# In-place low halves of q and k, u in the ring of x with R made per block, x issued by ScalarE, and one store of v for two heads

## The chip, the cores and the metric

The kernel runs on one core of a Trainium2 chip. The metric is the device time of one launch in microseconds (us). Engines are named as the profile names them: PE is the matrix engine (PEld its weight loads), DVE is VectorE, ACT is ScalarE, POOL is GpSimd, SP is SyncE. SPq and ACTq are the sequencers of SP and ACT when they issue a DMA.

## The reference

One layer with two branches over a sequence of 2048 tokens and 1024 channels. All float32.

```python
h = rms_norm(x, norm_gain)
z = h @ w_in                                  # 1024 -> 512+512+512+512+512+512+2048 columns
q, k, v, gate_a, u_s, gate_s, merge_logits = split(z)
q = rms_norm(q by heads of 64);  k = rms_norm(k by heads of 64)
o_a = diff_attention(q, k, v) * silu(gate_a)  # 4 heads of two sub-heads, block-causal, bias by distance
o_s = s5(u_s) * silu(gate_s)                  # 32 groups of a 64-state complex scan, gelu, glu
g_a, g_s = split(sigmoid(merge_logits + b))
x = x + (g_a * (o_a @ proj_attn) + g_s * (o_s @ proj_ssm)) @ w_out
```

## The kernel before, in words

**Arithmetic.** Each float32 operand of a matmul is split into a high part (a cast to the matmul's type) and a low part (what the cast lost), and a product is three matmuls: high by high (L40), high weight by low input (L41), low weight by high input (L42). `proj1` makes one output tile of 128 columns by 512 tokens out of 8 slices of channels, so 24 matmuls of 128x512. The helper `hilo` makes such a split: ACT casts (profile line L865), and DVE or POOL subtracts (L867).

**Phase 1** (`phase1`, 0 to about 444 us) works on four blocks of 512 tokens, t = 0 to 3. `load_x(t)` loads x in 8 tiles `xs` of 256 KB (DMA issued by SP at L180), makes hh and hl from them (L182, L183), and sums the squares into `acc` (L174, L176). From these come the statistics E (512 columns per block, in all partitions) and rc (per token). Then come four groups of projections, each over all four blocks:

- g = 0 and 1: two q tiles by `qk`, and between them four v tiles of 128 tokens by 256 columns by `value` (`ps_v`, 24 half-width matmuls each). The weights of v are loaded by `load_w` in raw tiles `wraw` (DMA issued by ACT at L134, cast L138, low part L139). In g = 0 the x of block t+1 is loaded in the same stretch.
- g = 2 and 3: two k tiles by `qk`, and between them two u tiles by `state` (`ps_u`), which DVE multiplies by R (from `newton` on E) and SP stores to US (L314).

The weights of `qk`, `state` and the gates come by `load_w1`: two raw tiles `wraw` per weight tile (DMA issued by ACT at L155), a cast on ACT (L159) and a subtraction on DVE (L160).

**`qk_norm`** finishes a pair of q or k tiles. It is called late, inside the next block's `qk` (`later`). Two matmuls with `bones` give the mean square `ms`; DVE adds E (`tt`, L237); `newton` makes the inverse root in place (ACT L94 and L95, DVE L96 to L98); DVE multiplies the two PSUM tiles by it (`q` and then `tt` itself, L243); each product is split into `qh` (ACT L865) and `ql` (DVE L867), and SP stores both (L246, L247), 256 KB each.

**After phase 1** `gate` computes 24 columns of gates and merge logits, 96 tiles `ps_p` with 24 matmuls each, to about 1020 us, while the preparation and the scan of the state-space branch run on DVE and POOL. Attention and the output projections follow.

**What sets the order.** The kernel is written on a scheduling layer that places each instruction in its engine's order when the kernel is built. At run time each engine takes its instructions strictly in that order and waits on semaphores. A tile with a `tag` lives in a ring of `bufs` buffers, and whoever takes a buffer again waits for its last reader, a store's landing included. The rings that matter here:

```python
BUFS = {"x": 4, "s": 2, "q": 2, "t": 2, "n": 2, "o": 2, "v": 2}
raw = k.wp.tile([128, 4, 128], F32, tag="wraw", bufs=3, name="wraw")     # in steps_w1
u = k.wp.tile([128, 8, 64], F32, tag="wraw", bufs=3, name="u")           # in state
wh, wl in load_w1: tag "wl" (4 buffers) unless "wh" (4 buffers, shared with the gates' z) is given
```

So `acc`, `tt` and `q` share the ring "t" of two buffers, `qh` and `ql` the ring "o" of two, and u shares three buffers with the raw weights.

Of the kernel before, what the change touches and what calls it, by code (L numbers as in the profile page):

```python
# [15 lines left out]
EPS = 1e-6  # L16
# [5 lines left out]
def f(ap):  # L22

    return ap.bitcast(F32)
# [54 lines left out]
def scratch(tc, k):  # L79
    d = k.dp  # L80
    k.QT, k.KT = ([d.tile([2, 2, 2, 64, T], F32R, name=f"{n}{i}") for i in range(2)] for n in "QK")
    k.QS, k.KS = ([x[h // 2][h % 2] for h in range(4)] for x in (k.QT, k.KT))
    k.VS = [d.tile([128, 16, 128], F32, name=f"VS{h}") for h in range(4)]
    k.US = [d.tile([128, 8, 256], F32, name=f"US{i}") for i in range(4)]
    k.SA = [d.tile([128, T], F32, name=f"SA{i}") for i in range(4)]
    k.SG = [d.tile([128, T], F32, name=f"SG{i}") for i in range(4)]
    k.TM = [d.tile([128, T], F32, name=f"TM{i}") for i in range(16)]
# [13 lines left out]
def phase1(tc, k, I, mid):  # L101

    nc = tc.nc
    with ExitStack() as es:
# [17 lines left out]
        def et(tag, name, dtype=F32):  # L122
            return k.ep.tile([128, TB], dtype, tag=tag, name=name, bufs=BUFS[tag])
# [42 lines left out]
        def load_x(t):  # L166

            acc = et("t", "acc")
            xs = {}
            lag = 2  # L170

            def square(kk):
                sq = acc if kk == 0 else et("q", "sq")
                nc.scalar.activation(out=sq, in_=xs[kk], func=AF.Square)  # L174
                if kk:
                    nc.gpsimd.tensor_tensor(out=acc, in0=acc, in1=sq, op=ALU.add)  # L176

            for kk in range(8):
                xs[kk] = et("x", "xs")
                nc.sync.dma_start(xs[kk], I["xT"][kk * 128:(kk + 1) * 128, t * TB:(t + 1) * TB])  # L180
                gc = k.gain[:, kk:kk + 1]
                nc.scalar.activation(out=hh[t][:, kk], in_=xs[kk], func=AF.Copy, scale=gc)  # L182
                nc.vector.scalar_tensor_tensor(out=hl[t][:, kk], in0=xs[kk], scalar=gc, in1=f(hh[t][:, kk]),  # L183
                                               op0=ALU.mult, op1=ALU.subtract)
                if kk >= lag:
                    square(kk - lag)
                yield
            for kk in range(8 - lag, 8):
                square(kk)
            ms = k.pF.tile([128, TB], F32, tag="F", bufs=k.NF, name="msx")  # L190
            sh, sl = et("s", "sh", F32R), et("s", "sl", F32R)
            hilo(nc, sh, acc, sl)
            nc.tensor.matmul(ms, k.ones, sh, start=True, stop=False)
            nc.tensor.matmul(ms, k.ones, sl, start=False, stop=True)
            e, r = E[:, t * TB:(t + 1) * TB], rc[:, 4 * t:4 * t + 4]
            nc.vector.tensor_scalar(out=e, in0=ms, scalar1=EPS / 1024, scalar2=EPS * EPS, op0=ALU.mult, op1=ALU.add)
            sq = et("q", "sq")
            for b in range(4):
                o = slice(128 * b, 128 * b + 128)
                nc.vector.tensor_tensor_reduce(out=sq[:, o], in0=e[:, o], in1=k.ident, scale=1.0, scalar=0.0,  # L200
                                               op0=ALU.mult, op1=ALU.add, accum_out=r[:, b:b + 1])
            newton(nc, k, k.cp, r, 4, r, EPS ** 0.5, ("rc_y", "rc_a"), 1)
            yield
# [28 lines left out]
        def qk_norm(t, gcol, dst, ps, sh, sl):  # L232
            ms = k.pF.tile([128, TB], F32, tag="F", bufs=k.NF, name="ms")
            nc.tensor.matmul(ms, k.bones, sh, start=True, stop=False)
            nc.tensor.matmul(ms, k.bones, sl, start=False, stop=True)
            tt = et("t", "tt")
            nc.vector.tensor_tensor(out=tt, in0=ms, in1=E[:, t * TB:(t + 1) * TB], op=ALU.add)  # L237
            newton(nc, k, k.ep, tt, TB, tt)
            ts = slice(t * TB, (t + 1) * TB)
            dst = dst.rearrange("h s l (i f) t -> i l (h s) f t", i=2)  # L240
            for i in range(2):
                q = et("t", "q") if i == 0 else tt
                nc.vector.scalar_tensor_tensor(out=q, in0=ps[i], scalar=gcol[:, i:i + 1], in1=tt, op0=ALU.mult, op1=ALU.mult)  # L243
                qh, ql = et("o", "qh", F32R), et("o", "ql", F32R)
                hilo(nc, qh, q, ql, nc.vector)
                nc.sync.dma_start(f(dst[i, 0, :, :, ts]), f(qh))  # L246
                nc.sync.dma_start(f(dst[i, 1, :, :, ts]), f(ql))  # L247

        def value(g, b):
            t, o = b // 4, (b % 4) * 128  # L250
            ps = pm.tile([128, 256], F32, tag="pm", name="ps_v")
            for kk in range(8):
                xh, xl = hh[t][:, kk, o:o + 128], hl[t][:, kk, o:o + 128]
                wh, wl = wk(g, kk)
                nc.tensor.matmul(ps, xh, wh, start=kk == 0, stop=False)  # L255
                nc.tensor.matmul(ps, xh, wl, start=False, stop=False)
                nc.tensor.matmul(ps, xl, wh, start=False, stop=kk == 7)
            v = k.ep.tile([128, 2, 128], F32, tag="v", bufs=BUFS["v"], name="v")
            nc.scalar.activation(out=v, in_=ps.rearrange("p (h d) -> p h d", h=2), func=AF.Copy, scale=rc[:, b:b + 1])  # L259
            for i in range(2):  # L260
                nc.sync.dma_start(k.VS[2 * (g - 4) + i][:, b], v[:, i])

        def steps(it, n=1):
            for _ in range(n):
# [3 lines left out]
        with ExitStack() as e1:  # L268
            k.ep = pool("ep", 1, e1)
            x = load_x(0)  # L270
            w2 = [steps_w1(i, "wh", nc.vector) for i in range(2)]
            w = [next(i) for i in w2]
            for i in range(4):
                steps(x)
                steps(w2[i // 2])
                steps(x)
            nc.sync.dma_start(k.ident, I["ident"])
            wv = load_w(4, nc.vector)
            for i in range(4):
                steps(wv)  # L280
                steps(x)
            for g in range(2):
                if g:
                    w = [load_w1(2 + i, "wh") for i in range(2)]
                    steps(load_w(5), 4)
                for t in range(NTB):
                    x = load_x(t + 1) if g == 0 and t + 1 < NTB else iter(())
                    n = (4, 0) if t == NTB - 1 else (2, 2)
                    b = iter(range(4 * t, 4 * t + 4))

                    def between(i):
                        for _ in range(n[i]):
                            steps(x, 2)
                            value(4 + g, next(b))
                        steps(x, 1 + 8 * i)

                    qk(w, t, k.qg, k.QT[g], between)

            RT = []
            for t in range(NTB):  # L300
                RT.append(et("x", "R"))
                newton(nc, k, k.ep, E[:, t * TB:(t + 1) * TB], TB, RT[t], EPS ** 0.5)
            for g in range(2, 4):
                w = [load_w1(2 * g + i, "wh") for i in range(2)]
                wu = [load_w1(12 + 2 * g + i) for i in range(2)]

                def state(i, t):

                    u = k.wp.tile([128, 8, 64], F32, tag="wraw", bufs=3, name="u")
                    ps = pm.tile([128, TB], F32, tag="pm", name="ps_u")  # L310
                    proj1(wu[i], t, ps)
                    v = lambda x: x.rearrange("p (c a) -> p c a", a=8)
                    nc.vector.tensor_tensor(out=u[:, ::-1].rearrange("p a c -> p c a"), in0=v(ps), in1=v(RT[t]), op=ALU.mult)
                    nc.sync.dma_start(k.US[2 * (g - 2) + i][:, :, 64 * t:64 * t + 64], u)  # L314

                for t in range(NTB):
                    def between(i):
                        if t < NTB - 1:
                            state(i, t)
                        elif i:  # L320
                            state(0, t)
                            state(1, t)

                    qk(w, t, k.kg, k.KT[g - 2], between)
            later()
            R = E
            for t in range(NTB):
                s = E[:, t * TB:(t + 1) * TB]
                newton(nc, k, k.ep, s, TB, s, EPS ** 0.5)
# [5 lines left out]

        def gate(c, ts, w=None, ps=pst):

            w = w or load_w1(c)
            for t in ts:
                if t == ts[0] or t % 2 == 0:  # L340
                    z, t0 = zt("z"), t
# [893 lines left out]
```

## Time and profile before

| what | value |
|---|---|
| median of three runs | 1801.59 us (1795.98 to 1806.88) |
| profiled execution: its time, and its span | 1796.61 us, 1794.8 us |
| PE, DVE, ACT, POOL busy | 95%, 57%, 39%, 16% of the span |
| granted PE clock, mean of the profiled execution | 0.979 |
| moved by DMA on the queue of SP / of ACT | 216.49 MB / 20.98 MB |

How to read it. The page's first parts give the busy time of each engine, and the span in 40 equal slices of 44.9 us with the busy share and the granted PE clock in tenths. The view of waits gives, for each kind of instruction, how long its engine stood idle before it and what ended that. The timeline lists instructions with start, duration, and the idle time before them in brackets. The view by windows gives the busy time and the number of instructions of each engine in a chosen stretch.

### The profile page before, as it was taken

What the parts mean: (1) busy time and instruction counts of PE and PEld (TensorE: products, weight loads), DVE (VectorE), ACT (ScalarE), POOL (GpSimd) and SP (SyncE); (2) the same over time, 40 slices, a digit from 0 to 9 for tenths busy, and PEclk for the clock granted to TensorE, in tenths of its full rate; (3) what the DMA queues carried; (4) which work ended last, traced back from release to release, by engine and by line L of the source; (5) the groups of instructions that cost most, each with busy time, mean ns of one, the idle gap of its engine ahead of it and who ended that gap; (6) DMA issues with size and microseconds to landing.
All of it is one profiled execution on the core that took longest, in us unless ns stands there. A gap on an engine that the chain in (4) does not pass through costs nothing.

```text
span 1794.8 us, 24838 instructions
## 1 busy us (share of the span) xinstructions
PE 1698.4 (95%) x8720; PEld 1434.5 (80%) x8720; DVE 1023.4 (57%) x2552; ACT 696.1 (39%) x1418; POOL 287.8 (16%) x428
## 2 busy tenths in 40 slices
PE   7878999897999999999999889999999989999998
PEld 6767988686887888888888778878888878888887
DVE  6432354434644339999745487688676668643331
ACT  4542232212411234331134576576555566511100
POOL 3320000000071000000013345552011032200000
PEclk9988999898999999999999989999999999999999
DMA  5323233423343443423355774763654443655532
GB/s 164 95 84 96 69 89 79 112 67 90 96 126 107 130 126 120 129 98 103 97 187 188 250 233 121 212 202 110 206 176 131 146 129 105 209 156 154 152 100 83
DMA packets 225916, 239.04 MB, mean 133 GB/s; under 512 B 56544, under 2 KB 166528, under 8 KB 224768
## 3 DMA queue, kind: packets, MB, share of 16 engines
q1 hardware_dynamic: 186624, 216.49, 40.0%
q10 hardware_dynamic: 39168, 20.98, 4.1%
q8 instruction: 69, 1.13, 0.3%
q14 instruction: 55, 0.45, 0.1%
HBM read 146.44 MB, written 90.96 MB: 132 GB/s over the span
## 4 chain that ended last, share of the span: by engine, by line
PE 62%; DMA 14%; DVE 6%; ACT 4%; POOL 3%; issue 2%; SPq 1%; ACTq 0%; DVEq 0%; POOLq 0%
PE ps_p L40 9%; PE ps_p L41 9%; PE ps_p L42 9%; PE ps_o L576 4%; DMA K<-ql 3%; PE ps_o L41 3%; PE ps_o L42 3%; PE ps_o L40 3%; PE ps_s L536 2%; PE ps_s L537 2%; PE ps_t L568 2%; PE ps_a L40 2%; PE ps_a L41 1%; PE ps_qk L40 1%; PE ps_a L42 1%
## 5 line engine op out<-in xcount | busy, mean ns | idle before, releaser
L40 PE MATMUL ps_p<-hh,w 128*128 128x512 f32 x768 | 302.2, 394 | 9.5 <-ACT w L159 9.5
L41 PE MATMUL ps_p<-hl,w 128*128 128x512 f32 x768 | 302.0, 393 | 0.0
L42 PE MATMUL ps_p<-hh,w 128*128 128x512 f32 x768 | 300.8, 392 | 0.0
L40 PEld LDWEIGHTS ps_p<-hh,w 128*128 128x128 f32 x768 | 145.4, 189 | 39.5 <-ACT w L159 9.9
L41 PEld LDWEIGHTS ps_p<-hl,w 128*128 128x128 f32 x768 | 145.3, 189 | 30.1 <-issue 0.4
L42 PEld LDWEIGHTS ps_p<-hh,w 128*128 128x128 f32 x768 | 145.0, 189 | 29.5 <-issue 0.7
L549 ACT ACTIVATE e<-e,mm 128x640 f32<-128x640 f32 (+11 forms) x96 | 136.3, 1420 | 64.5 <-DVE mm L547 64.1
L576 PE MATMUL ps_o<-V,at 128*128 128x128 f32 x1088 | 149.3, 277 | 1.0 <-ACT sq L582 0.7
L576 PEld LDWEIGHTS ps_o<-V,at 128*128 128x128 f32 x1088 | 142.2, 193 | 8.7 <-ACT sq L582 1.9
L539 DVE TENSOR_SCALAR_CACHE_REDUCE e<-ps_s 128x512 f32<-128x512 f32 (+1 forms) x192 | 120.5, 641 | 29.4 <-PE ps_s L537 28.1
L536 PE MATMUL ps_s<-K,Q 128*128 128x512 f32 (+3 forms) x320 | 128.9, 405 | 2.9 <-DVE e L539 2.2
L537 PE MATMUL ps_s<-K,Q 128*128 128x512 f32 (+3 forms) x320 | 116.5, 366 | 6.2 <-DMA Q<-Q 6.2
L40 PE MATMUL ps_qk<-hh,w 128*128 128x512 f32 x256 | 102.8, 402 | 17.4 <-ACT w L159 8.8
L345 DVE TENSOR_TENSOR z<-ps_p,E 128x512 f32<-128x512 f32 x96 | 65.9, 687 | 70.6 <-PE ps_p L42 69.9
L41 PE MATMUL ps_qk<-hl,w 128*128 128x512 f32 x256 | 102.5, 400 | 3.7 <-DVE hl L183 3.7
L42 PE MATMUL ps_qk<-hh,w 128*128 128x512 f32 x256 | 101.5, 396 | 0.0
L255 PE MATMUL ps_v<-w,hh 128*128 128x256 f32 x256 | 77.3, 304 | 22.9 <-ACT v L259 13.5
L351 ACT ACTIVATE z<-z,hmb 128x512 f32<-128x512 f32 x64 | 46.3, 724 | 118.7 <-DVE z L345 113.9
L559 DVE SCALAR_TENSOR_TENSOR e<-e,cf 128x128 f32<-128x128 f32 (+7 forms) x64 | 89.9, 1405 | 1.3
L568 PE MATMUL ps_t<-ident,e 128*128 128x128 f32 x544 | 84.2, 274 | 5.0 <-ACT at L570 2.1
L570 ACT COPY at<-ps_t 128x512 f32<-128x512 f32 (+3 forms) x160 | 78.4, 519 | 18.4 <-PE ps_t L568 18.2
L542 DVE CUSTOM_DVE_ANT_0 e<-ps_s,nb 128x384 f32<-128x384 f32 (+3 forms) x128 | 69.7, 552 | 17.9 <-PE ps_s L537 17.1
(346 smaller groups left out, 3684.8 us busy)
## 6 DMA issues: line engine op xcount, KB each, us to landing
wraw<-win ACTq DMA_DIRECT2D x80, 256.0 KB
TM<-z SPq DMA_DIRECT2D x32, 512.0 KB
xs<-xT SPq DMA_DIRECT2D x32, 256.0 KB
u<-US SPq DMA_DIRECT2D x64, 128.0 KB
K<-K SPq DMA_DIRECT2D x8, 1024.0 KB
Q<-Q SPq DMA_DIRECT2D x32, 256.0 KB
Q<-Q SPq DMA_DIRECT2D x64, 128.0 KB
t<-TM SPq DMA_DIRECT2D x32, 256.0 KB
```

Of the source, the lines that this page charges most:

```text
L40: nc.tensor.matmul(out, wh, xh, start=start, stop=False)
L41: nc.tensor.matmul(out, wh, xl, start=False, stop=False)
L42: nc.tensor.matmul(out, wl, xh, start=False, stop=stop)
L255: nc.tensor.matmul(ps, xh, wh, start=kk == 0, stop=False)
L536: nc.tensor.matmul(ps, Q[:, 0, s, 128 * b:128 * b + 128], Kt[s][:, ks], start=True, stop=False)
L537: nc.tensor.matmul(ps, Q[:, 1, s, 128 * b:128 * b + 128], Kt[s][:, ks], start=False, stop=True)
L539: nc.vector.tensor_scalar(out=et[:, ks], in0=ps, scalar1=0.0, scalar2=3e38, op0=ALU.add, op1=ALU.min, accum_out=mc[:, i:i + 1])
L549: nc.scalar.activation(out=et, in_=et, func=AF.Exp, bias=mm, scale=-1.0, accum_out=su)
L559: nc.vector.scalar_tensor_tensor(out=e[0], in0=e[1], scalar=cf, in1=e[0], op0=ALU.mult, op1=ALU.add)
L568: nc.tensor.transpose(pt[:, x], e[:, o:o + 128], k.ident)
L570: nc.scalar.copy(AT[g][:, :w], pt[:, :w])
L576: nc.tensor.matmul(po, AT[x // 4][:, x % 4], Vt[x // 8][:, x % 8], start=x == 0, stop=x == n - 1)
```

## The change

Four edits, all in phase 1 but for the ring of the first gate's weights. Lines from L83 on stand one later in the changed kernel, from L262 on up to four earlier; `hilo`'s cast is L864 there.

- The low half of q or k is written over the product itself (`hilo` without a separate low tile), and the store reads it there. `qh` then has the ring "o" to itself, and `q` and `tt` (ring "t") are held until their stores have landed.
- x of the blocks t = 1 to 3 is issued by ACT in place of SP.
- v of two heads goes to DRAM in one store of 128 KB in place of two of 64 KB.
- u takes its buffer from the ring "x" (free after the last x) in place of "wraw". R is no longer made for all four blocks ahead of g = 2 but per block within g = 2 and again within g = 3, 8 calls of `newton` in place of 4. The first gate's weights take the ring "wh".

```diff
-    k.VS = [d.tile([128, 16, 128], F32, name=f"VS{h}") for h in range(4)]
+    k.VT = [d.tile([2, 128, 16, 128], F32, name=f"VT{i}") for i in range(2)]
+    k.VS = [k.VT[h // 2][h % 2] for h in range(4)]
...
-                nc.sync.dma_start(xs[kk], I["xT"][kk * 128:(kk + 1) * 128, t * TB:(t + 1) * TB])
+                (nc.scalar if t else nc.sync).dma_start(xs[kk], I["xT"][kk * 128:(kk + 1) * 128, t * TB:(t + 1) * TB])
...
-                qh, ql = et("o", "qh", F32R), et("o", "ql", F32R)
-                hilo(nc, qh, q, ql, nc.vector)
+                qh = et("o", "qh", F32R)
+                hilo(nc, qh, q, eng=nc.vector)
                 nc.sync.dma_start(f(dst[i, 0, :, :, ts]), f(qh))
-                nc.sync.dma_start(f(dst[i, 1, :, :, ts]), f(ql))
+                nc.sync.dma_start(f(dst[i, 1, :, :, ts]), q)
...
-            for i in range(2):
-                nc.sync.dma_start(k.VS[2 * (g - 4) + i][:, b], v[:, i])
+            nc.sync.dma_start(k.VT[g - 4][:, :, b].rearrange("h p d -> p h d"), v)
...
-            RT = []
-            for t in range(NTB):
-                RT.append(et("x", "R"))
-                newton(nc, k, k.ep, E[:, t * TB:(t + 1) * TB], TB, RT[t], EPS ** 0.5)
...
-                    u = k.wp.tile([128, 8, 64], F32, tag="wraw", bufs=3, name="u")
+                    u = et("x", "u").rearrange("p (a c) -> p a c", a=8)
...
-                    nc.vector.tensor_tensor(..., in1=v(RT[t]), op=ALU.mult)
+                    nc.vector.tensor_tensor(..., in1=v(R), op=ALU.mult)
...
                 for t in range(NTB):
+                    R = et("x", "R")
+                    newton(nc, k, k.ep, E[:, t * TB:(t + 1) * TB], TB, R, EPS ** 0.5)
+
...
-            w = w or load_w1(c)
+            w = w or load_w1(c, "wh" if c == cols[0] else "wl")
```

**Order on ACT at the change from g = 2 to g = 3.** `wraw_2774` and `wraw_2778` are the two raw halves of the first k weights of g = 3, `w1_2772` the tile cast from them, `qh_2678` the last split of a `qk_norm` in g = 2 (of its third block), `nw_y_2872` the `newton` of the fourth. Before:

```order
L217 ACTIVATE sq_2709<-ps_qk_2684 128x512
L865 CAST qh_2671<-q_2669 128x512
L865 CAST sh_2768<-sq_2655 128x512
L865 CAST qh_2678<-tt_2660 128x512
L155 DMA wraw_2774<-win 128x4x128
L155 DMA wraw_2778<-win 128x4x128
L94 ACTIVATE nw_y_2872<-tt_2870 128x512
L159 CAST w1_2772<-wraw_2774 128x512
L95 ACTIVATE nw_y_2872<-nw_y_2872 128x512
L159 CAST w1_2772<-wraw_2778 128x512
```

After, the same weights are `wraw_2718`, `wraw_2722` and `w1_2716`. ACT issues their loads while the first block of g = 2 is worked on:

```order
L864 CAST qh_2047<-tt_2030 128x512
L156 DMA wraw_2120<-win 128x4x128
L156 DMA wraw_2718<-win 128x4x128
L864 CAST sh_2080<-sq_1913 128x512
L156 DMA wraw_2722<-win 128x4x128
L160 CAST w1_2114<-wraw_2120 128x512
L218 ACTIVATE sq_2157<-ps_qk_2132 128x512
```

and casts them some thirty rows later, ahead of the square of the last block's first k tile (`ps_qk_2576`):

```order
L864 CAST qh_2497<-q_2495 128x512
L864 CAST qh_2503<-tt_2486 128x512
L864 CAST sh_2564<-sq_2453 128x512
L160 CAST w1_2716<-wraw_2718 128x512
L160 CAST w1_2716<-wraw_2722 128x512
L218 ACTIVATE sq_2601<-ps_qk_2576 128x512
```

So the loads moved by three blocks, and the casts from behind the last `newton` of g = 2 to the middle of its last block.

**Order on PE at the start of the gates.** `ms` is the last mean square of k, `w1_5740` and `w1_5741` (after: `w1_5706`, `w1_5707`) are the high and low weights of the first gate, `ps_p` the gates' tiles. Before:

```order
L235 MATMUL ms_3380<-sl_3377,bones_72 128x512
L40 MATMUL ps_p_5751<-hh0_155,w1_5740 128x512
L41 MATMUL ps_p_5751<-hl0_156,w1_5740 128x512
L40 MATMUL ps_p_5778<-hh1_150,w1_5740 128x512
L41 MATMUL ps_p_5778<-hl1_151,w1_5740 128x512
L40 MATMUL ps_p_5807<-hh2_145,w1_5740 128x512
```

After:

```order
L236 MATMUL ms_3348<-sl_3345,bones_72 128x512
L40 MATMUL ps_p_5717<-hh0_153,w1_5706 128x512
L41 MATMUL ps_p_5717<-hl0_154,w1_5706 128x512
L42 MATMUL ps_p_5717<-hh0_153,w1_5707 128x512
L40 MATMUL ps_p_5717<-hh0_153,w1_5706 128x512
L41 MATMUL ps_p_5717<-hl0_154,w1_5706 128x512
```

Before, the first slice of weights is spread over four tiles ahead of its low half; after, one tile's 24 matmuls follow each other. On ACT the loads and casts of these weights moved as those above did: before, `wraw_5742` and `wraw_5746` stand behind the last split of g = 3's third block; after, the loads stand at the start of g = 3 and the casts ahead of the first square of its last block.

**Order on ACT in g = 0, while block 2 is worked on and x of block 3 is loaded.** `acc_832` (after: `acc_820`) is the first square of block 3, `xs` and `hh3` are block 3's, `qh_655` and `qh_662` (after: `qh_647`, `qh_653`) are the high halves of block 0's q, `tt_921` (after: `tt_907`) is block 1's. Before:

```order
L865 CAST qh_655<-q_653 128x512
L217 ACTIVATE sq_830<-ps_qk_805 128x512
L865 CAST qh_662<-tt_644 128x512
L174 ACTIVATE acc_832<-xs_833 128x512
L94 ACTIVATE nw_y_764<-rc_158 128x4
L174 ACTIVATE sq_879<-xs_837 128x512
L95 ACTIVATE nw_y_764<-nw_y_764 128x4
L174 ACTIVATE sq_915<-xs_870 128x512
L182 ACTIVATE hh3_140<-xs_911,small_77 128x512
L94 ACTIVATE nw_y_923<-tt_921 128x512
L259 ACTIVATE v_866<-ps_v_841,rc_158 128x256
```

After:

```order
L260 ACTIVATE v_854<-ps_v_829,rc_156 128x256
L260 ACTIVATE v_894<-ps_v_869,rc_156 128x256
L175 ACTIVATE acc_820<-xs_821 128x512
L181 DMA xs_956<-xT 128x512
L183 ACTIVATE hh3_138<-xs_897,small_77 128x512
L95 ACTIVATE nw_y_909<-tt_907 128x512
L175 ACTIVATE sq_901<-xs_857 128x512
L96 ACTIVATE nw_y_909<-nw_y_909 128x512
L183 ACTIVATE hh3_138<-xs_956,small_77 128x512
L181 DMA xs_963<-xT 128x512
L218 ACTIVATE sq_954<-ps_qk_929 128x512
L183 ACTIVATE hh3_138<-xs_963,small_77 128x512
```

The first two copies of v moved ahead of the square that opens the next block's statistics, and the loads of x now stand between ACT's own work. `acc_820` takes the buffer of block 0's `q`, `tt_907` that of block 0's `tt`, and both buffers are now read by a store. The next copy of v (`v_995`) stands right behind these rows. On SP the four stores of a block (two `qh`, then `q` and `tt`) now follow each other, no x stands among them, and each v tile has one row in place of two.

More of the change, by code (lines that the diff above doesn't have):

```diff
@@ L312, in state @@
                     v = lambda x: x.rearrange("p (c a) -> p c a", a=8)
-                    nc.vector.tensor_tensor(out=u[:, ::-1].rearrange("p a c -> p c a"), in0=v(ps), in1=v(RT[t]), op=ALU.mult)
+                    nc.vector.tensor_tensor(out=u[:, ::-1].rearrange("p a c -> p c a"), in0=v(ps), in1=v(R), op=ALU.mult)
                     nc.sync.dma_start(k.US[2 * (g - 2) + i][:, :, 64 * t:64 * t + 64], u)
                 for t in range(NTB):
+                    R = et("x", "R")
+                    newton(nc, k, k.ep, E[:, t * TB:(t + 1) * TB], TB, R, EPS ** 0.5)
                     def between(i):
```

## The prediction

> **What bounds the kernel now.** I read the page's head and slices first, then counts by windows, then PE's waits, and then the timeline around each of PE's gaps, following each gap back. The page:
>
> ```profile
> span 1794.8 us, 24838 instructions
> PE   7878999897999999999999889999999989999998
> PEclk9988999898999999999999989999999999999999
> ```
>
> PE is the bound, and short of full mostly in the first eleven slices, which are phase 1. How much is missing there, by windows (columns: window, its length, then busy us and instructions of PE, PEld, DVE, ACT, POOL, then the granted PE clock, the DMA share and GB/s):
>
> ```profile
> 40.00:120.00 80.00, 61.28 (x341) 53.09 (x339) 33.02 (x61) 38.34 (x70) 28.53 (x22) 0.91 0.33 92
> 120.00:175.00 55.00, 43.48 (x235) 38.92 (x236) 21.26 (x38) 16.07 (x31) 5.58 (x5) 0.84 0.33 89
> 240.00:320.00 80.00, 80.00 (x354) 66.11 (x353) 43.58 (x65) 25.25 (x43) 0.00 (x0) 1.00 0.30 78
> 320.00:360.00 40.00, 31.19 (x130) 25.03 (x129) 16.47 (x24) 8.76 (x15) 0.00 (x0) 0.87 0.44 117
> 420.00:460.00 40.00, 30.50 (x124) 24.63 (x123) 17.09 (x25) 8.94 (x16) 0.00 (x0) 0.87 0.42 111
> 600.00:1000.00 400.00, 400.00 (x1887) 331.89 (x1886) 267.05 (x776) 138.18 (x267) 30.74 (x40) 1.00 0.43 133
> ```
>
> In 240 to 320 PE never stops: 354 matmuls in 80 us, 0.226 us each, so 177 in 40 us. Around 340 it does 130 and around 440 it does 124. These two holes cost (177 - 130) x 0.226 = 10.6 us and (177 - 124) x 0.226 = 12.0 us, the slower clock behind each hole included (0.87). From 40 to 175 half-width matmuls of v are mixed in, so the count doesn't serve. Idle time plus the share lost to the clock gives 18.7 + 0.09 x 61.3 = 24 us before 120 and 11.5 + 0.16 x 43.5 = 18.5 us behind it. The same reckoning gives 8.8 + 0.13 x 31.2 = 12.9 us at 340, where the count says 10.6; scaled by that, 20 and 15 us. In 600 to 1000 PE is full, so what phase 1 gives up should reach the gates' end whole.
>
> PE's waits in phase 1 (the line that waited, what ended it, us, times, the longest):
>
> ```profile
> PE ps_v L255 <- ACT v L259: 13.5, 3, 8.1
> PE ps_p L40 <- ACT w L159: 9.5, 1, 9.5
> PE ps_qk L40 <- ACT w L159: 8.8, 1, 8.8
> PE ps_v L255 <- ACT w L138: 8.4, 2, 6.5
> ```
>
> **The two holes at 340 and 440: u, R and the rings.** Timeline of the first, and the start of the second:
>
> ```profile
> 330.47 0.62 ACT L865 CAST qh<-tt 128x512 fp32r<-128x512 f32 x1 [5.27 <-DMA K<-qh]
> 330.55 0.38 ACTq L155 DMA_DIRECT2D wraw<-win  x1
> 333.08 0.69 DVE L867 TENSOR_TENSOR ql<-tt,qh 128x512 fp32r<-128x512 f32 x1 [7.05 <-DMA K<-ql]
> 334.77 2.87 SPq L314 DMA_DIRECT2D US<-u  x2
> 342.16 0.63 ACT L94 ACTIVATE nw_y<-tt 128x512 f32<-128x512 f32 x1 [11.07 <-DMA US<-u]
> 343.35 0.79 PE L40 MATMUL ps_qk<-hh,w 128*128 128x512 f32 x1 [8.81 <-ACT w L159]
> 444.12 0.79 PE L40 MATMUL ps_p<-hh,w 128*128 128x512 f32 x1 [9.50 <-ACT w L159]
> ```
>
> The chain that ended last (start, us, what) says what ACT stood for:
>
> ```profile
> 325.46 7.53 DMA K<-ql
> 334.77 6.82 DMA US<-u
> 341.74 0.37 ACTq L155
> ```
>
> The low half waits for an earlier store of a low half, u stands behind it on DVE, its store takes 6.8 us, and only then is a buffer of "wraw" free. ACT's second raw load (341.74) stands in ACT's order behind that, and the cast behind the load; PE waits for the cast. With u in the ring of x, no raw load waits for a store of u: the order shows the loads three blocks earlier and the cast ahead of a square after which PE still has 72 matmuls (one k tile and two of u), 16.3 us, against two casts (0.62 each, as the cast above) and two subtractions (0.69), 2.6 us. The hole goes: **-10.6**. At the gates the order moves the same way, with the first gate's weights in "wh", whose former tiles are free once the last k tile's matmuls are done: **-12.0**. If the last slice of weights were still late I would expect 1 to 3 us of each back, so -8 to -10.6 and -9 to -12. Next late at those points is the last `newton` of a group, which holds PSUM tiles only.
>
> R per block adds 4 calls of `newton` (8 for 4): two passes of 0.63 on ACT and three on DVE.
>
> ```profile
> 303.45 0.69 DVE L96 TENSOR_TENSOR nw_a<-nw_y,tt 128x512 f32<-128x512 f32 x1 [1.36 <-ACT nw_y L95]
> 324.35 0.51 SPq L246 DMA_DIRECT2D K<-qh  x1
> ```
>
> That is 1.3 us of ACT and 2.1 of DVE per block of 96 matmuls (21.7 us), where ACT is busy 25.25 of 80 us and DVE 43.58 of 80: hidden, **0** (if DVE's cover were gone, at most 4 x 2.1 = 8.4 us).
>
> **Low halves in place.** The passes are the same in number; what changes is who waits for stores. `ql`'s waits on its own stores and the wait of the second `qh` go; in their place `tt` waits until the last block's `q` has landed, and `q` until its `tt` has. Is that cycle longer than a block? From `ms`: add 0.69, `newton` 1.3 + 2.1, two products 1.5, first cast 0.6: the first store leaves at about +6.2. A store issued at 324.35 had landed when ACT went on at 330.47 (6.1 us), the one issued at 325.46 at 332.99, 2.5 us behind it. So the third of four, `q`, lands at 6.2 + 6.1 + 2 x 2.5 = +17.3, or +20.7 if one of the two US stores (6.82 us the pair, 3.4 each) gets between. Against 21.7 that is in time, **0** in the steady stretches, which PE runs through at full already.
>
> **The first loss, 40 to 120: x, and the first in-place lows.**
>
> ```profile
> 84.60 0.67 SPq L246 DMA_DIRECT2D Q<-qh  x1
> 86.83 0.52 SPq L247 DMA_DIRECT2D Q<-ql  x1
> 91.33 0.62 ACT L865 CAST qh<-tt 128x512 fp32r<-128x512 f32 x1 [4.93 <-DMA Q<-qh]
> 91.97 0.51 SPq L246 DMA_DIRECT2D Q<-qh  x1
> 92.58 0.97 SPq L180 DMA_DIRECT2D xs<-xT  x2
> 95.10 0.51 SPq L247 DMA_DIRECT2D Q<-ql  x1
> 99.53 0.72 ACT L182 ACTIVATE hh<-xs,small 128x512 fp32r<-128x512 f32 x1 [4.35 <-DMA xs<-xT]
> 101.15 1.75 SPq L261 DMA_DIRECT2D VS<-v  x4
> 101.18 0.58 PE L255 MATMUL ps_v<-w,hh 128*128 128x256 f32 x1 [8.15 <-ACT v L259]
> ```
>
> ACT waits for a store at 91.33, SP issues x behind the next store, ACT's hh waits for that x until 99.53, and the copy of v that PE needs stands behind hh. In the changed kernel `qh` doesn't wait and two copies of v stand ahead, so PE gets two more v tiles (48 half-width matmuls, 48 x 0.113 = 5.4 us). But then `acc_820` waits for the landing of `q`: with the first store at 84.6 landing at 91.3 (ACT went on at 91.33) and 2.5 us for each further one, 91.3, 93.8, 96.3, 98.8; `acc_820` at 96.3, `tt_907` at 98.8. Behind `acc_820` on ACT stand the issue of x, hh, another issue, hh, and then the copy `v_995` that PE needs next: 97 for the first issue, 3 to 7 us for a load (99.53 - 92.58 is 6.95), the second issue behind that: `v_995` between 104 and 110. Before, PE had these two v tiles done at 101.2 + 5.4 = 106.6. So **0** is my value, between -9 (the whole 8.15 goes with its clock) and +5 (ACT's wait on a store, 4.93, is simply added).
>
> The 24 issues that ACT takes over cost 0.38 each by its own row above, 9 us in 100 where ACT is busy under half. SP loses them, and 32 issues of v (1.75 / 4 = 0.44 each, 14 us over phase 1); nobody waits for SP's sequencer in these rows, only for what it queues behind stores: 0.
>
> A rule of the Trainium skill speaks against the x edit: "DMA: Bandwidth & Descriptors", section "Issuing engines are not separate DMA queues", says that DMAs started by different engines end on the same 16 DMA engines and that issuing from several saves only the issue time. By it this stretch stays at 0 and the sum as below; were x free of the stores ahead of it, it would go towards -9. The row at 92.58 shows x slow behind a store, and cannot tell a queue from a shared engine.
>
> **The second loss, 120 to 175: weights of g = 1.**
>
> ```profile
> 138.70 0.47 ACT L259 ACTIVATE v<-ps_v,rc 128x256 f32<-128x256 f32 x1 [5.04 <-DMA VS<-v]
> 151.42 0.69 DVE L867 TENSOR_TENSOR ql<-tt,qh 128x512 fp32r<-128x512 f32 x1 [11.01 <-DMA Q<-ql]
> 153.85 0.62 ACT L138 CAST w<-wraw 128x512 fp32r<-128x512 f32 x1 [4.41 <-DVE w L160]
> 154.52 0.79 PE L255 MATMUL ps_v<-w,hh 128*128 128x256 f32 x2 [6.47 <-ACT w L138]
> 159.24 0.58 PE L255 MATMUL ps_v<-w,hh 128*128 128x256 f32 x1 [1.93 <-ACT w L138]
> ```
>
> DVE stands 11.01 us for a store of a low half, the weights' low halves (L160) stand behind it on DVE, ACT's next load and cast behind them, PE behind the cast. The in-place low half has no such wait. PE's two gaps, 8.4 of 11.5 us idle, are 8.4 / 11.5 x 15 = 11 us with their clock; some comes back since `tt_1206`, ahead of all this on DVE, now waits for a store of block 1. I take **-10**, between -15 (all of it) and +5 (ACT's wait of 5.04 on a store of v comes on top).
>
> **Sum** against the profiled execution (1796.6): -10.6 - 12.0 - 10 + 0 = -32.6, so 1764.0. The median of the runs, 1801.59, stands 5.0 above that execution, which would make 1769. I write 1767.
>
> **Rivals.**
>
> (a) x gets free of the stores and all early loss goes: -22.6 - 20 - 15 = -58, 1739; with half of the first loss 1751. For it: hh's wait at 99.53. Against it: the new waits of `acc_820` and `tt_907`, worked out above. Chance 0.12.
>
> (b) Only the two holes go; in 120 to 175 the new waits of `tt` cost what `ql`'s gave: 1774. Chance 0.20.
>
> (c) Slower: the ring "t" becomes the block's clock. If both US stores and the v or R work get ahead, `q` lands at 17.3 + 6.8 + some 3 of DVE delay = +27, 5.5 us past the block, and each of the eight k blocks waits as long: +44, 1808. The gain is eaten from 32.6 / 8 = 4.1 us past the block on. Against it: before, `ql` waited about 7 us in every such block and PE ran at full in 240 to 320. Chance 0.07.
>
> (d) The gain is lost behind the gates, where the state-space branch on DVE must be done when attention begins: half lost is 1780, all lost 1797. DVE's 267 busy of 400 us speaks against. Chance 0.13.
>
> (e) The raw loads don't move in effect (they wait for their ring anyway), 1797: the order speaks against it. Chance 0.03.
>
> **How the numbers follow.** The forecast, 1755 to 1772 by its bounds, has 0.45. 0.5% (9 us) is about what a measurement of this kernel can tell from no change. Faster: 0.45 + 0.12 + 0.20 + 0.05 of (d) = 0.82; same: 0.08 of (d) + 0.03 = 0.11; slower 0.07. The range 1742 to 1786 takes in the forecast, (b), half of (a) and the milder part of (d): about 0.8.
>
> **What would show it.** Right: around 340 and 440 no PE wait on L160 (`w`) above 1 us and 175 or more matmuls per 40 us; no wait of a raw load on US; the gates' start some 30 us earlier; ACT's `acc` and DVE's `tt` waiting for stores of `q` and `tt` in g = 0. Wrong: `tt` waiting for stores in g = 2 and 3 with PE idle there; or a hole at the new weights of g = 1 as long as before; or PE idle between the gates and attention by what was gained.

## The result and the profile after

The changed kernel takes 1773.01 us (median of 4 runs, 1772.84 to 1774.31) against 1799.92 for the kernel before in the same runs: ratio 0.9848, 95% interval 0.9816 to 0.988. That is 27 us; a second series later gave 0.9852 (0.9831 to 0.9873). The forecast was 1767, in a range from 1742 to 1786. Between the two profiled executions the spans differ by 23.6 us; the one of before stands at the fast end of its runs.

The page's head and slices of the changed kernel:

```profile
span 1771.2 us, 24819 instructions
PE   7877999999999999999999789999999989999999
PEclk9888999999999999999999899999999999999999
```

The dents in slices 8 and 10 of before are gone. By windows (columns as before):

```profile
40.00:120.00 80.00, 63.37 (x342) 54.54 (x340) 32.86 (x62) 39.17 (x70) 28.99 (x22) 0.89 0.35 95
120.00:175.00 55.00, 45.60 (x257) 40.42 (x258) 21.41 (x39) 17.54 (x33) 5.59 (x5) 0.88 0.31 90
320.00:360.00 40.00, 40.00 (x178) 33.07 (x177) 22.61 (x34) 12.26 (x22) 0.00 (x0) 1.00 0.43 113
420.00:460.00 40.00, 40.00 (x178) 33.13 (x177) 27.35 (x101) 20.76 (x26) 0.00 (x0) 1.00 0.33 101
600.00:1000.00 400.00, 392.57 (x1841) 326.77 (x1840) 272.47 (x781) 143.70 (x282) 35.84 (x48) 0.99 0.45 142
```

Both holes are closed: 178 matmuls in 40 us, at full clock. The first two windows hardly changed.

Where the time came from is read off landmarks. The view of a tile gives, for a group of matmuls, their shortest, median and longest duration in ns and the first and last start in us. Before:

```profile
L255 PE MATMUL ps_v<-w,hh x256: 274/283/582, 17.2 to 238.6; 128*128 128x256 f32 x128
L40 PE MATMUL ps_u<-hh,w x128: 389/389/499, 250.3 to 433.3; 128*128 128x512 f32 x128
L40 PE MATMUL ps_p<-hh,w x768: 387/389/792, 444.1 to 1020.1; 128*128 128x512 f32 x192
L536 PE MATMUL ps_s<-K,Q x320: 220/398/667, 1020.8 to 1538.9; 128*128 128x512 f32 x92, 128*128 128x384 f32 x60, 128*128 128x128 f32 x4, 128*128 128x256 f32 x4
```

After:

```profile
L256 PE MATMUL ps_v<-w,hh x256: 274/283/582, 18.2 to 234.7; 128*128 128x256 f32 x128
L40 PE MATMUL ps_u<-hh,w x128: 389/389/389, 246.5 to 418.4; 128*128 128x512 f32 x128
L40 PE MATMUL ps_p<-hh,w x768: 387/389/504, 419.5 to 986.8; 128*128 128x512 f32 x192
L535 PE MATMUL ps_s<-K,Q x320: 221/399/774, 990.3 to 1515.4; 128*128 128x512 f32 x92, 128*128 128x384 f32 x60, 128*128 128x128 f32 x4, 128*128 128x256 f32 x4
```

The last v starts 3.9 us earlier, the last u 14.9, the first gate 24.6, the last scores of attention 23.5, and the end is 23.6 earlier. Both traces hold 8720 matmuls, so the lead can also be read between the n-th matmul of one and the n-th of the other. It is 24.6 us at the first gate, 27.3 from 200 matmuls later on, 30.3 another 300 matmuls on, behind a stop of PE in the state-space preparation that is 3.2 us long in the kernel before (`ps_w`, see e1), 29.8 at matmul 4560 near the end of the gates, 25.0 at matmul 5040 in attention, and 23.2 at the end. So the stretch before 240 gave 3.9, the hole at 340 gave 11.0, the one at 440 gave 9.7 by its stop and 2.7 by its clock (12.0 by the count), the shorter stop at `ps_w` gave 3.0, and about 5 of these 30 went again where attention begins.

### The profile page after: what moved, and what is told of

Read it like the earlier page. It is cut to its first block, busy times and chain, and to the rows that moved or that the text cites. A ratio compares the mean times of both kernels' runs of the same rounds, so it can differ in the third digit from the quotient of the medians.

```text
span 1771.2 us, 24819 instructions
## 1 busy us (share of the span) xinstructions
PE 1691.9 (96%) x8720; PEld 1426.8 (81%) x8720; DVE 1032.2 (58%) x2564; ACT 699.7 (40%) x1426; POOL 285.8 (16%) x428
## 4 chain that ended last, share of the span: by engine, by line
PE 70%; DMA 13%; DVE 7%; ACT 3%; POOL 3%; issue 3%; SPq 1%; ACTq 0%; POOLq 0%; DVEq 0%
PE ps_p L40 9%; PE ps_p L41 9%; PE ps_p L42 9%; PE ps_o L575 5%; PE ps_o L40 3%; PE ps_o L42 3%; PE ps_o L41 3%; PE ps_s L536 2%; PE ps_s L535 2%; PE ps_qk L40 2%; PE ps_qk L41 2%; PE ps_qk L42 2%; PE ps_t L567 2%; DMA xs<-xT 2%; PE ps_u L42 1%
## 5 line engine op out<-in xcount | busy, mean ns | idle before, releaser
L567 PEld LDWEIGHTS ps_t<-ident,e 128*128 128x128 f32 x544 | 65.7, 141 | 22.0 <-ACT at L569 6.0
```

The costliest lines, as they stand in the source:

```text
L567: nc.tensor.transpose(pt[:, x], e[:, o:o + 128], k.ident)
```

## The experiments

Each was timed against the kernel before in the same series. Besides the ratios, the landmarks and waits of their profiles decide.

**e1: u's ring, R per block and the first gate's ring alone, on the kernel before.**

```diff
...
-                    u = k.wp.tile([128, 8, 64], F32, tag="wraw", bufs=3, name="u")
+                    u = et("x", "u").rearrange("p (a c) -> p a c", a=8)
...
                 for t in range(NTB):
+                    R = et("x", "R")
+                    newton(nc, k, k.ep, E[:, t * TB:(t + 1) * TB], TB, R, EPS ** 0.5)
...
-            w = w or load_w1(c)
+            w = w or load_w1(c, "wh" if c == cols[0] else "wl")
```

> The kernel before with one part of the change alone: u in the ring of x, R made per block, the first gate's weights in the ring wh. Theory (the two holes at 340 and 440 are the raw loads that wait for u's stores, and the other parts hardly move the end): both holes go, about 22 us, some 3 of it lost again behind the gates, so 18 to 23 us under the kernel before, near 1779; the first 175 us as before, with DVE standing about 11 us for a store of ql at 151. Rival (the holes close only because the low halves in place free the queue of stores): at least one hole stays with more than 5 us, and the time is above 1787.

Measured: 1791.01 us, ratio 0.9938 (0.992 to 0.9956), 11 us. Both holes are gone, as the theory has it (first row: 420 to 460), yet half of what they were worth is missing. It stands in PE's waits from 440 to 620 (second row), in DVE's and ACT's waits from 395 to 560 and in DVE's timeline:

```profile
420.00:460.00 40.00, 40.00 (x178) 33.13 (x177) 15.94 (x23) 14.49 (x20) 0.00 (x0) 1.00 0.33 91
```

```profile
PE ps_w L829 <- DVE wn L700: 13.3, 1, 13.3
```

```profile
DVE ql L866 <- DMA K<-ql: 19.4, 3, 7.0
DVE big L700 <- POOL cp L700: 17.6, 1, 17.6
ACT qh L864 <- DMA K<-qh: 17.0, 3, 6.2
```

```profile
451.58 0.69 DVE L866 TENSOR_TENSOR ql<-tt,qh 128x512 fp32r<-128x512 f32 x1 [5.75 <-DMA K<-ql]
```

`ps_w` is a transpose in the state-space preparation that stands 436 matmuls (98.7 us at 0.226) behind the first gate in PE's order; `wn` is made by DVE from POOL's `cp`. With the first gate at 426.5, PE is there at 525.2 and `wn` comes at 538.4. Matmul by matmul, e1 leads the kernel before by 20.3 us ahead of this stop and by 10.1 behind it. The same waits in the kernel before and in the changed kernel:

```profile
PE ps_w L830 <- DVE wn L701: 3.2, 1, 3.2
DVE big L701 <- POOL cp L701: 9.9, 1, 9.9
```

```profile
PE ps_w L829 <- DVE wn L700: 1.5, 2, 0.9
DVE big L700 <- POOL cp L700: 5.2, 1, 5.2
```

In the kernel before, the hole gave DVE the time; in the changed kernel something else did. e5 and e9 ask what.

**e2: all but u's ring** (low halves in place, x by ScalarE, v in one store, on the kernel before).

> The change without u's ring, R per block and the first gate's ring: only the low halves in place, x by ScalarE and v in one store. Theory: the first 235 us end about 4 us earlier, as in the changed kernel, and both holes stay, since u's store still stands between the raw loads and their buffers: 2 to 6 us under the kernel before, near 1796. Rival (in-place lows let u be stored sooner, so the holes shrink): the hole at 340 under 5 us and the time under 1788.

Measured: 1802.18 us, ratio 1.0001 (0.9985 to 1.0018): no change. Both holes stay, by PE's waits up to 500:

```profile
PE ps_p L40 <- ACT w L160: 9.0, 1, 9.0
PE ps_qk L40 <- ACT w L160: 8.9, 1, 8.9
```

The last v starts at 233.4, 5.2 us earlier than before, but the end isn't earlier: near the end of the gates e2 still leads the profiled kernel before by 8.7 us, and at its end it is 4.3 behind. That is lost in attention, whose code is the same but for the place of v in DRAM; why isn't shown. So the two halves of the change give 0.6% and nothing, and together 1.5%.

**e5: the changed kernel with the separate `ql`.**

```diff
-                qh = et("o", "qh", F32R)
-                hilo(nc, qh, q, eng=nc.vector)
+                qh, ql = et("o", "qh", F32R), et("o", "ql", F32R)
+                hilo(nc, qh, q, ql, nc.vector)
...
-                nc.sync.dma_start(f(dst[i, 1, :, :, ts]), q)
+                nc.sync.dma_start(f(dst[i, 1, :, :, ts]), f(ql))
```

> The changed kernel with the separate low tile ql back in the ring o, as before; u's ring, R per block, x by ScalarE and v in one store stay. Theory (in e1 DVE's waits of ql at the end of phase 1 made the state-space preparation late, and PE stood 13.3 us for wn at its first ps_w; the low halves in place are what takes this wait away): the wait for wn is back with 8 to 15 us, 7 to 16 us over the changed kernel, 1780 to 1789. Rival (x or v are what saves that time): under 2 us over the changed kernel, and the wait for wn stays under 3 us.

Measured: 1792.31 us, ratio 0.9928 (0.9909 to 0.9947), against 0.9848 for the changed kernel some 14 us more. Against e7, which is the changed kernel but for v's stores and ran in the same series, it is 18.8 us, and the profiled spans are 19.2 apart (1790.4 and 1771.2), so the loss is at the upper end of the theory's 7 to 16 or above it. The wait is back, and x and v don't take it away:

```profile
PE ps_w L829 <- DVE wn L700: 12.4, 1, 12.4
```

The last v starts at 241.3 here, 6.6 us later than in the changed kernel; the first gate (426.1) is 6.6 later too, the first `ps_w` (537.6 against 519.4) 18.2. So 6.6 us of the difference stand in the early stretch and 11.6 in this wait.

**e9: low halves in place in g = 3 alone.**

```diff
+            last = dst is k.KT[1]
...
-                qh = et("o", "qh", F32R)
-                hilo(nc, qh, q, eng=nc.vector)
+                qh, ql = et("o", "qh", F32R), None if last else et("o", "ql", F32R)
+                hilo(nc, qh, q, ql, nc.vector)
...
-                nc.sync.dma_start(f(dst[i, 1, :, :, ts]), q)
+                nc.sync.dma_start(f(dst[i, 1, :, :, ts]), q if last else f(ql))
```

> The changed kernel with the low halves in place only in g = 3 (the last group of k); g = 0 to 2 keep a separate ql. Theory (what e5 lost lies mostly in DVE's waits of ql at the end of phase 1, which make wn late): PE's wait for wn falls from 12.4 us to under 4, the first 240 us stay as in e5 (6 us later than the changed kernel), and the time is 1776 to 1782. Rival (the low halves in place matter through the early stretch, and the wait for wn comes from elsewhere, such as POOL's cp): the wait for wn stays above 8 us and the time above 1786.

Measured: 1777.09 us, ratio 0.9858 (0.9837 to 0.9879), the changed kernel's own within the intervals. The wait fell as the theory said, with the early stretch still late (last v at 239.0):

```profile
PE ps_w L830 <- DVE wn L701: 1.9, 1, 1.9
```

So four blocks of k at the end of phase 1 carry most of what the low halves in place are worth. What they change there is seen in the changed kernel's waits from 395 to 560, where ACT's `qh` no longer waits for a store of K and DVE waits for them in this row alone:

```profile
DVE tt L238 <- DMA K<-q: 10.0, 2, 6.5
```

In e1 it was 19.4 us on DVE and 17.0 on ACT. DVE's first instruction of the state-space preparation (a MEMSET of `P`) starts at 449.1 in the changed kernel, 29.6 us behind the first gate, and at 468.4 in e1, 41.9 us behind it. So `wn` comes in time for a PE that no longer stops in the first, and too late in the second.

**e3: the squares' sum in E's own slice, on the changed kernel.** It takes `acc` out of the ring "t".

```diff
-            acc = et("t", "acc")
+            acc = E[:, t * TB:(t + 1) * TB]
```

> The changed kernel with the sum of squares of a block built in that block's own slice of E in place of a buffer of the ring t, so that only tt and q share that ring. Theory (what the early stretch failed to give was taken by the new waits of acc and tt for stores, 7.8 us on ACT at 98, 11.3 and 8.6 us on DVE at 100 and 134): ACT's wait of acc is gone, PE's stop of 6.4 us at 106 goes or falls under 2 us, the raw loads of g = 1 start sooner, and the time falls by 6 to 15 us, to 1758 to 1767. Rival (x comes late or the raw loads bound that stretch whatever acc does): less than 3 us.

The waits it is aimed at, in the changed kernel's timeline:

```profile
97.91 0.63 ACT L175 ACTIVATE acc<-xs 128x512 f32<-128x512 f32 x1 [7.78 <-DMA Q<-q]
100.55 0.69 DVE L238 TENSOR_TENSOR tt<-ms,E 128x512 f32<-128x512 f32 x1 [11.29 <-DMA Q<-tt]
106.00 0.46 ACT L260 ACTIVATE v<-ps_v,rc 128x256 f32<-128x256 f32 x1
106.51 0.80 PE L40 MATMUL ps_qk<-hh,w 128*128 128x512 f32 x1 [6.37 <-ACT v L260]
133.94 0.69 DVE L238 TENSOR_TENSOR tt<-ms,E 128x512 f32<-128x512 f32 x1 [8.60 <-DMA Q<-q]
134.67 0.63 ACT L95 ACTIVATE nw_y<-tt 128x512 f32<-128x512 f32 x1 [8.42 <-DVE tt L238]
145.82 0.62 ACT L139 CAST w<-wraw 128x512 fp32r<-128x512 f32 x1 [4.83 <-DMA wraw<-win]
153.08 0.62 ACT L139 CAST w<-wraw 128x512 fp32r<-128x512 f32 x1 [4.29 <-DMA wraw<-win]
153.75 0.80 PE L256 MATMUL ps_v<-w,hh 128*128 128x256 f32 x2 [4.86 <-ACT w L139]
```

Read down: ACT stands for the landing of `q`; the copy of v that PE needs comes at 106; in the next block DVE's `tt` stands for `q` again, ACT for `tt`, and the raw weights of g = 1, which ACT issues behind that, come late for PE.

Measured: 1757.02 us, ratio 0.9751 (0.9732 to 0.9771), the fastest kernel of this study and a little beyond the theory's 6 to 15 us. ACT's wait of `acc` and PE's stop at 106 are gone. The windows of e3:

```profile
40.00:120.00 80.00, 66.78 (x392) 58.66 (x390) 38.86 (x67) 39.68 (x72) 29.45 (x22) 0.91 0.36 103
120.00:175.00 55.00, 51.65 (x299) 46.01 (x300) 21.52 (x40) 18.73 (x37) 5.16 (x4) 0.97 0.33 97
```

The last v starts at 219.6, 15.1 us earlier than in the changed kernel; the second window, 0.88 of the clock in the changed kernel, has 0.97. PE's busy time times its clock shows where the gain lies: 60.8 against 56.4 us in the first window (66.78 x 0.91, 63.37 x 0.89), 50.1 against 40.1 in the second.

**e10: the same on the kernel before**, as a control.

> The kernel before with the squares' sum in E, as in e3. Theory (e3's gain is the removal of waits that the low halves in place brought into the ring t, which the kernel before doesn't have): within 5 us of the kernel before. Rival (a ring with one user less helps whatever the low halves do): 8 us or more under the kernel before.

Measured: 1794.93 us against 1802.86, ratio 0.9957 (0.9941 to 0.9974), 8 us: the bound that I had given the rival. So e3's 1% over the changed kernel isn't all the removal of waits that the low halves brought; up to 8 us come from a ring with one user less in either kernel. The landmarks and the windows part the shares. Up to the last v the edit gives 5.4 us here (233.2 against 238.6) and 15.1 in the changed kernel:

```profile
40.00:120.00 80.00, 68.31 (x383) 60.54 (x382) 37.22 (x64) 38.76 (x71) 26.55 (x20) 0.89 0.37 96
120.00:175.00 55.00, 43.94 (x226) 38.02 (x225) 19.45 (x37) 16.73 (x32) 8.11 (x6) 0.88 0.33 93
```

Busy time times clock gains 5.0 us over the kernel before in the first window, about as much as e3 gains over the changed kernel there, and 2.2 in the second, where e3 gains 10.0. So it is the second window in which the new waits cost.

**e6: the changed kernel with x issued by SP, and e8: e3 with x issued by SP.**

```diff
-                (nc.scalar if t else nc.sync).dma_start(xs[kk], ...)
+                nc.sync.dma_start(xs[kk], ...)
```

> The changed kernel with x issued by SP in all blocks, as before. Theory (where x is issued is worth nothing by itself, since acc and tt wait for the stores anyway): within 3 us of the changed kernel, 1770 to 1776. Rival (x behind the stores on SP's queue is what cost the early stretch): 5 to 12 us over it, and ACT's hh waits for x with single waits of 4 us or more.

> The kernel of e3 (the squares' sum in E) with x issued by SP as before. Theory: with acc no longer waiting, x is the next thing that can be late; behind the four stores of a block on SP's queue it lands later, so 3 to 10 us over e3, 1760 to 1767. Rival (x's queue is worth nothing here either, since the DMA engines are shared): within 2 us of e3.

Measured: e6 1768.96, ratio 0.9803 (0.9779 to 0.9828), a little under the changed kernel's two ratios (0.9848 and 0.9852, of other series) and within the intervals of e7 in its own series (0.9819). The profiles agree that x by ScalarE is worth nothing that can be told there: with x issued by SP the first gate starts 1.1 us earlier than in the changed kernel, and most of the 8.2 us between the two spans lies in attention, which the edit doesn't touch. e8 1768.56, ratio 0.9789 (0.9764 to 0.9815), against 0.9751 for e3: there it gains some 0.4%, 7 us, as the theory said, and the first gate of e8 starts 7.5 us later than that of e3 (411.9 and 404.4). The same edit has no fixed price; it is worth something once `acc` no longer holds ACT. The first x tile of block 3, its issue and the `hh` made from it, in e3 and then in e8:

```profile
72.19 0.33 ACTq L181 DMA_DIRECT2D xs<-xT  x1
78.27 0.72 ACT L183 ACTIVATE hh<-xs,small 128x512 fp32r<-128x512 f32 x1 [0.77 <-DMA xs<-xT]
```

```profile
74.33 2.90 SPq L261 DMA_DIRECT2D VT<-v  x1
77.31 1.07 SPq L181 DMA_DIRECT2D xs<-xT  x1
86.46 0.72 ACT L183 ACTIVATE hh<-xs,small 128x512 fp32r<-128x512 f32 x1 [7.12 <-DMA xs<-xT]
```

Issued by ACT at 72.19, the tile is there for `hh` at 78.27, after 6.1 us. SP issues it at 77.31, behind Q's four stores and a store of v whose issue alone took 2.9 us, and it is there at 86.46, after 9.1 us. So `hh` is 8.2 us later: 5.1 by the later issue and 3.1 by the slower landing. The Trainium skill's "DMA: Bandwidth & Descriptors", section "Issuing engines are not separate DMA queues", has it that another issuer saves only the issue time. The larger part here, 5.1 us, agrees with that; the 3.1 us of landing aren't issue time, and whether they come from the queue or from the neighbours in those microseconds wasn't measured.

**e4: the first gate's weights in "wl"**, on the changed kernel, and **e7: v in two stores**.

```diff
-            w = w or load_w1(c, "wh" if c == cols[0] else "wl")
+            w = w or load_w1(c)
```

> The changed kernel with the first gate's weights in the ring wl, as before; the rest of the change stays. Theory: it is the release of the raw ring that closes the hole at 440, but the weights then need buffers that the last u tiles of g = 3 still read, so that the casts must come after u's last matmuls: a hole of 3 to 6 us at the start of the gates, 1776 to 1780. Rival (the raw loads alone matter): no hole, 1773.

> The changed kernel with v stored in two transfers of 64 KB, as before. Theory (nobody waits for SP's issue time): within 2 us of the changed kernel. Rival (the longer chain of issues between Q's stores delays their landing, which acc and tt now wait for): 3 to 8 us over it.

Measured: e4 1776.25, ratio 0.9859 (0.9839 to 0.9879); no hole, so the theory's mechanism fell, though 1776 lies in its range, and the rival held: moving u out of "wraw" closes the hole without the ring "wh". Against the changed kernel's 0.9848 and 0.9852 nothing can be told.

```profile
420.00:460.00 40.00, 40.00 (x178) 33.11 (x178) 28.01 (x100) 21.70 (x28) 0.00 (x0) 1.00 0.38 113
```

e7 1773.52, ratio 0.9819 (0.9795 to 0.9842): the single store of v is worth nothing that can be told.

**e11: e3 with a third buffer for v.**

> The kernel of e3 with three buffers for v in place of two. ACT waited 10.9 us in three pieces for stores of v between 40 and 240 us in e3. Theory (PE has no stop left there that ends in v but 3.4 and two short ones of 0.9 to 2 us): within 3 us of e3, 1754 to 1759. Rival (those waits hold the loads of x and of the weights behind them): 4 to 10 us under e3.

Measured: 1761.89, ratio 0.9765 (0.9742 to 0.9788), e3's (of another series) within the intervals. ACT's waits for stores of v vanish from the view of waits, and nothing comes of it.

**e12: the changed kernel again.**

> The changed kernel itself beside the others of this call, for a ratio against the same runs of the kernel before: 0.982 to 0.988 of the kernel before; PE's wait for wn under 3 us, ACT's wait of acc near 8 us, as in its first profile.

Measured: 1776.37, ratio 0.9852 (0.9831 to 0.9873); ACT's wait of `acc` 7.7 us. Its ratio is the one to hold e9 against.

## Why the prediction was right or wrong

**The two holes: sizes right, cause right, cover missed.** The forecast took 10.6 and 12.0 us; the landmarks show 11.0 and 12.4. That the raw loads waited for u's stores is shown by e1 and e2: with u moved the holes go, with all the rest but u they stay. The failed step is "Next late at those points is the last `newton` of a group, which holds PSUM tiles only". What is late next is `wn`: with the hole at 440 closed, PE came to `ps_w` 13.3 us early (e1), and the credit of -22.6 to u's ring held only because the low halves in place had freed DVE (e5, e9). In the sum the low halves in the k blocks had 0; by e5 against the changed kernel they are worth 14 to 19 us with all groups, and by e9 most of that is in g = 3. That the whole credit reached the end of the gates was luck as far as the working goes: both edits happened to be made together.

**The first loss, 40 to 120: right.** The forecast had `acc` waiting until 96.3, `tt` until 98.8, `v_995` between 104 and 110, and 0 in all. The trace has 97.91, 100.55 and 106.00; the second `msx` of that stretch starts at 118.89 against 119.18 before. Rival (a) is excluded: the early loss didn't go, and the wait named against it stands in the timeline ahead of PE's stop. That this wait alone is the cause isn't shown: e10 gains as much in this window in the kernel before, where `acc` waits for no store of `q`.

**The second loss, 120 to 175: size off.** The term was -10, and the whole stretch up to the last v gave 3.9. `ql`'s wait of 11.01 went, but the new wait of `tt` for the store of `q`, named with "some comes back", is 8.60 on DVE and 8.42 on ACT, and the raw loads of g = 1 stand behind it on ACT. PE's waits for the weights of v only fell from 8.4 to 6.8 us, so the sign of being wrong, a hole there as long as before, nearly came. The step counted how much of the wait went and not what stands behind the new one. e3 shows what more was to be had here: some 10 us.

**The block's clock (rival c): landing right, block wrong.** I had `q` landing at +17.3 to +20.7 of a block of 21.7. DVE's waits from 235 to 445 in the changed kernel:

```profile
DVE tt L238 <- DMA K<-q: 16.8, 3, 6.9
```

The longest of these ends at 316.45, when the `q` of the block before has landed, 19.4 us behind the end of that block's `ms` (297.05): as worked out. What was wrong is the 21.7. The last block of a group has both its u tiles behind its second k tile, so that the `ms` aren't evenly spaced. Their second matmul starts at 296.66, 313.47, 341.17, 363.42, 385.67, 402.49 and 419.30: 16.8 us apart three times, and 27.7 once. In the short blocks `q` lands too late, `tt` starts 2 to 4 us behind its `ms`, and the rest of DVE's wait is time in which `ms` wasn't there either. PE's slack took it (178 matmuls in 320 to 360). The rival was nearer than its price said.

**Behind the gates:** the lead of 29.8 us at matmul 4560 is 25.0 at matmul 5040, as if rival (d) had come in a mild form. The other profiles speak against it. In all of them 2.6 to 7.8 us of the lead over the profiled kernel before go in these 480 matmuls, whatever the lead is: 5.0 of 45.2 in e3, 7.8 of 9.6 in e1, 3.4 of 7.8 in e10. A chain on DVE that doesn't move with the gates would take more from a larger lead. It fits better that the one profiled execution of the kernel before passed this stretch quickly; with a single profile of it that isn't shown.

**x, v and R at 0:** v holds (e7). x holds in this kernel, and not as a rule (e8). R per block was run only together with u's ring; PE doesn't stop in 320 to 360 or 420 to 460, so it costs nothing there.

The measured 27 us against the forecast 33 is thus: holes as forecast, second loss 6 short, 3 gained at `ps_w` that no term had, and some 5 lost again at the start of attention, with the spread of the kernel before's runs (1795.98 to 1810.47 over all series) on top. By the number alone 1773 is rival (b)'s 1774, and it lies a little above the forecast's own interval of 1755 to 1772; by the mechanism it is between the two, since 3.9 of the 10 us came. That interval was also narrower than the working: the bounds of the terms add up to 1750 and 1790. In rival (a), half of the first loss gives 1749 and not 1751.

## What to carry to other kernels

When a stop of the bounding engine is closed, look in its order for the next instruction that waits for another engine, and work out when each gets there: a hole can be the cover of a late chain, and then two edits that give 0.6% and nothing give 1.5% together. Storing from the tile that was computed in, in place of a copy, lengthens that tile's hold on its ring until the store has landed; every other user of the ring (here a sum of squares that had nothing to do with it) then waits for that store, so give such users another place, as e3 did for 1% more, about a third of which the same edit gave in the kernel before too (e10).

## What was unexpected of the hardware

The same load of 256 KB took 6.1 us from another engine's queue and 9.1 us behind four stores on their own queue (e3, e8), in a stretch (40 to 120) where the DMA engines' mean busy share was about a third. How much of the difference is the queue, and how much the different neighbours in those microseconds, wasn't measured. Issuing itself was slow behind those stores: the store of v that came next occupied SP for 2.9 us, the one after it for 0.38 (e8, at 74.33 and 78.85).
